# RWKV-7 recursion in a fused transformer block: heads in the two column halves of TensorE's array, two pairs of heads per visit

## The chip, the cores and the metric

The kernel runs on one core of a Trainium2 chip. A core has TensorE (PE; matrix products into PSUM, each with a weight load, PEld), VectorE (DVE), ScalarE (ACT), GpSimd (POOL) and SyncE (SP), which here issues nearly all DMAs. The engines run beside each other and wait for one another by semaphores. The metric is device microseconds of one execution; before the change the median of three runs was 1608.07 us (1606.12 to 1613.35).

## The reference

One layer of an encoder trunk on 256 tokens of width 2048, all in float32: an input projection, two attentions of four heads (stick-breaking and forgetting), an RWKV-7 time mixing with sixteen heads of 64, gated branch products, an output projection and a squared-ReLU MLP of width 8192. What matters here is the recursion of each RWKV head:

```
def frame(state, inp):
    r_t, w_t, k_t, v_t, kk_t, kka_t = inp
    sa = einsum('bhvk,bhk->bhv', state, kk_t)
    state = state * w_t - sa[..., None] * kka_t + v_t[..., None] * k_t
    return state, einsum('bhvk,bhk->bhv', state, r_t)
```

It is a scan over 256 tokens with a 64x64 state in each head.

## The kernel before, in words

**The weight stream.** All large products (GEMMs) read weights in pieces of 128x1024 float32 by DMA. ACT copies each piece to a rounded high part (`whi`, L138), DVE takes the remainder (`wlo`, L139), and TensorE multiplies both parts. In the stage of this change the GEMM is `tok` (L212 for most of it, L197 for the tail of a group): gate and branch products with the tokens in the output's rows. A piece gives eight products with `whi` and four with `wlo`, each 128x128 by 128x512.

**The mixers.** Attention and recursion are a generator, `mixers`, whose pieces are laid between the GEMM's products. `tok` calls `tick` after every four products with `whi` of one weight tile and after every two with `wlo`; `tick` adds credit, and while there is credit it runs the generator up to the next `yield`. A yield ("stage", cost) takes the cost off the credit and ends the tick; I call the work between two such yields a *visit*. When the GEMMs that may go beside the mixers are used up, `while not fin[0]: step()` issues what is left with no ticks. A scheduler then lists each engine's instructions in the order in which it expects them to be ready, so neighbouring pieces can still be shuffled on an engine.

**The recursion.** It runs in two halves of eight heads, four pairs of heads each (`rwkv_half`, PR is the list of pairs). The 256 tokens are cut into four chunks of 64, so a half has 32 triangular systems of 64x64, one for each head and chunk. `SC` holds for each system the score products, `Xt` the values (rows 64 to 128) and the solution (rows 0 to 64), `Bt` and `Kt` the decayed keys and receptances, `Pb` the state of a pair as a block-diagonal 128x128 matrix.

1. DVE inverts the 32x32 diagonal blocks of all systems. Two products of 32x32 per system put the off-diagonal block in place (L626, L633), sixteen systems per visit, four visits; each visit's results are copied by one ACT instruction (L627, L634).
2. Chunk by chunk, five visits for the right-hand sides and the solutions: visit j forms pair j's right-hand side from the state (L652, 64 columns of the array, both heads at once) and the values (L656, per head), and applies the inverse to the right-hand side of pair j-1 (L659, per head). ACT copies both (L662 into `rh`, L664 into `Xt`).
3. Then four visits, one for each pair: the state's update (L670) and the output (L673 from the state, L675 from the solution), each on the whole array for both heads, of whose 128x128 results only the two diagonal 64x64 blocks are used. ACT scales the state (L678), DVE adds the blocks (L682, L684), ACT copies the output blocks (L688).

In a chunk that makes nine visits with a credit of 5 x 0.3 + 4 x 0.6 = 3.9.

Of the kernel before, what the change touches and what calls it, by code (L numbers as in the profile page):

```python
# [49 lines left out]
def hybrid_block(ctx, tc, xt, x, gains, params, consts, lora, gup, wst, out):  # L50
# [244 lines left out]
    ps = mps()  # L295
# [181 lines left out]
    def rwkv_half(hf):  # L477
# [144 lines left out]
        for q in range(2):  # L622
            ps = mps()
            for j in range(16):
                sl = 16 * q + j
                PE.matmul(ps[32:64, j * 32:j * 32 + 32], SC[0:32, sl, 32:64], TW[0:32, sl, :], start=True, stop=True)  # L626
            A.activation(TW[32:64, 16 * q:16 * q + 16, :], ps[32:64].rearrange("p (a b) -> p a b", a=16), AF.Copy)  # L627
            yield ("stage", 0.1)
        for q in range(2):
            ps = mps()  # L630
            for j in range(16):
                sl = 16 * q + j
                PE.matmul(ps[0:32, j * 32:j * 32 + 32], TW[32:64, sl, :], SC[32:64, sl, 32:64], start=True, stop=True)  # L633
            A.activation(SC[0:32, 16 * q:16 * q + 16, 32:64], ps[0:32].rearrange("p (a b) -> p a b", a=16), AF.Copy)  # L634
            yield ("stage", 0.1)
# [7 lines left out]
        for c in range(4):  # L643
            sls = {p: [i * 8 + h * 4 + c for h in range(2)] for i, p in enumerate(PR)}
            rhs = {}

            for j in range(5):
                p, o = PR[j] if j < 4 else None, PR[j - 1] if j else None
                psr = mps() if j < 4 else None
                pso = mps() if j else None  # L650
                if c and j < 4:
                    PE.matmul(psr[0:64, 0:128], Bt[p][:, c, 0:64], Pb[p], start=True, stop=False)  # L652
                for h in range(2):
                    hc = slice(64 * h, 64 * h + 64)
                    if j < 4:
                        PE.matmul(psr[0:64, hc], SC[64:128, sls[p][h], 0:64], Xt[p][64:128, c, hc],  # L656
                                  start=c == 0, stop=c == 0 or h == 1)
                    if j:
                        PE.matmul(pso[0:64, hc], SC[0:64, sls[o][h], 0:64], rhs[o][:, hc], start=True, stop=True)  # L659
                if j < 4:  # L660
                    rhs[p] = rp.tile([64, 128], F32, tag="rh", name=nm("rh"), bufs=4)
                    A.activation(rhs[p], psr[0:64, 0:128], AF.Copy)  # L662
                if j:
                    A.activation(Xt[o][0:64, c, :], pso[0:64, 0:128], AF.Copy)  # L664
                yield ("stage", 0.3)
            for i, p in enumerate(PR):
                X = Xt[p]
                if c < 3:
                    ps = mps()
                    PE.matmul(ps[:, 0:128], Kt[p][:, c, :], X[:, c, :], start=True, stop=True)  # L670
                ps2 = mps()
                if c:
                    PE.matmul(ps2[:, 0:128].rearrange("p (a b) -> p a b", a=2), Pb[p],  # L673
                              Bt[p][:, c:c + 1, 64:128].to_broadcast([128, 2, 64]), start=True, stop=False)
                PE.matmul(ps2[:, 0:128].rearrange("p (a b) -> p a b", a=2), X[:, c, :],  # L675
                          SC[:, sls[p][0]:sls[p][1] + 1:4, 64:128], start=c == 0, stop=True)
                if 0 < c < 3:
                    A.activation(Pb[p], Pb[p], AF.Copy, scale=ecol[:, i, c:c + 1])  # L678
# [7 lines left out]
                for h in range(2):  # L686
                    hr = slice(64 * h, 64 * h + 64)
                    A.activation(y[p][hr, c * 64:c * 64 + 64], ps2[hr, hr], AF.Copy)  # L688
# [580 lines left out]
```

## Time and profile before

| | us |
|---|---|
| median of three runs | 1608.07 |
| the profiled execution | 1608.3 |
| its span, first to last instruction | 1606.5 |
| PE busy | 1562.1 (97%) |
| DVE busy | 1194.4 (74%) |
| ACT busy | 926.7 (58%) |
| first 32x32 product (L626) of the first half | 353.8 |
| first 32x32 product of the second half | 594.9 |

The profile is one execution. PE's rows are matrix products, which are pipelined, so the distance between two starts tells more than their lengths. A float32 product of the recursion appears as two weight loads and two MATMUL records of the same line; I call one such record with its load a *step*. In the trace's rows "64*64" is the part of the array in use (rows times columns), the next figure the output's size in partitions and elements moved. "128*64 128x128" for L652 so means 128 rows and 64 columns of the array with 128 elements moved. Times count from the first instruction.

### The profile page before, as it was taken

How to read it: one execution, taken by the hardware profiler on the slowest of the kernel's cores; microseconds unless marked ns; L12 is line 12 of the kernel's file. 1: busy time of each engine (PE TensorE's matmuls, PEld its weight loads, DVE VectorE, ACT ScalarE, POOL GpSimd, SP SyncE). 2: the span in 40 equal slices, each digit the busy share in tenths (PEclk: the TensorE clock that was granted, in tenths of full speed). 3: DMA queues.
4: the chain of work that ended last, by engine and by line, in shares of the span. 5: the costliest groups of instructions: out<-in, count | busy, mean ns of one | idle time of the engine just before them, and what ended most of it. 6: DMA issues, size and time to landing. Idle time of an engine off the chain costs nothing.

```text
span 1606.5 us, 23353 instructions
## 1 busy us (share of the span) xinstructions
PE 1562.1 (97%) x8846; PEld 1317.1 (82%) x8846; DVE 1194.4 (74%) x1591; ACT 926.7 (58%) x1408; POOL 45.3 (3%) x104
## 2 busy tenths in 40 slices
PE   7999999999999999999999999999899998999997
PEld 7999999997777887788887888887688777878785
DVE  7764558874577884555555778899999999899755
ACT  7474476545675445744444766666666665666442
POOL 0030001000001000000000000000000000000000
PEclk9999999999999999999999999999999999999998
DMA  6646444453445453365685565665466655656564
GB/s 235 209 132 194 148 154 160 148 177 105 136 150 173 156 172 114 103 196 194 204 293 171 169 186 170 209 197 180 164 209 196 202 169 181 200 193 210 168 191 138
DMA packets 94144, 283.38 MB, mean 176 GB/s; under 512 B 9296, under 2 KB 11600, under 8 KB 94032
## 3 DMA queue, kind: packets, MB, share of 16 engines
q1 hardware_dynamic: 91200, 280.66, 53.8%
q8 instruction: 69, 1.13, 0.3%
q10 hardware_dynamic: 2832, 1.24, 0.3%
q14 instruction: 43, 0.35, 0.1%
HBM read 279.77 MB, written 2.10 MB: 175 GB/s over the span
## 4 chain that ended last, share of the span: by engine, by line
PE 83%; DVE 10%; ACT 3%; issue 3%; POOL 1%; DMA 1%; DVEq 0%; SPq 0%; POOLq 0%; ACTq 0%
PE gps L212 29%; PE gps L154 10%; PE gps L197 6%; PE gps L156 6%; PE gps L175 5%; PE gps L176 5%; PE gps L180 5%; DVE wlo L139 3%; DVE raw L1015 2%; PE mps L1047 2%; PE mps L1049 2%; PE mps L1048 2%; ACT whi L138 2%; PE gps L1047 1%; PE gps L1048 1%
## 5 line engine op out<-in xcount | busy, mean ns | idle before, releaser
L139 DVE TENSOR_TENSOR wlo<-raw,whi 128x1024 fp32r<-128x1024 f32 x590 | 716.0, 1222 | 285.6 <-ACT whi L138 235.9
L138 ACT ACTIVATE whi<-raw 128x1024 fp32r<-128x1024 f32 x590 | 619.9, 1057 | 438.0 <-PE gps L212 175.6
L212 PE MATMUL gps<-whi,pk 128*128 128x512 f32 x1144 | 295.4, 396 | 0.0
L212 PEld LDWEIGHTS gps<-whi,pk 128*128 128x128 f32 x1144 | 210.7, 188 | 45.5 <-issue 2.5
L154 PE MATMUL gps<-pk,whi 128*128 128x512 f32 x960 | 244.8, 391 | 0.2 <-ACT whi L138 0.2
L154 PEld LDWEIGHTS gps<-pk,whi 128*128 128x128 f32 x960 | 178.2, 188 | 37.6 <-ACT whi L138 1.1
L212 PE MATMUL gps<-wlo,pk 128*128 128x512 f32 x572 | 160.7, 395 | 0.0
L156 PEld LDWEIGHTS gps<-pk,wlo 128*128 128x128 f32 x1024 | 139.1, 190 | 13.8 <-DVE wlo L139 4.7
L175 PE MATMUL gps<-pk,whi 128*128 128x256 f32 x584 | 148.2, 290 | 0.0
L156 PE MATMUL gps<-pk,wlo 128*128 128x256 f32 x1024 | 143.5, 283 | 1.7 <-DVE wlo L139 1.7
L176 PE MATMUL gps<-pk,whi 128*128 128x256 f32 x584 | 144.5, 283 | 0.0
L212 PEld LDWEIGHTS gps<-wlo,pk 128*128 128x128 f32 x572 | 105.3, 188 | 22.0 <-issue 0.8
L1015 DVE TENSOR_TENSOR raw<-raw,raw 128x1024 f32<-128x1024 f32 x96 | 117.0, 1219 | 0.8
L175 PEld LDWEIGHTS gps<-pk,whi 128*128 128x128 f32 x584 | 112.0, 192 | 2.3 <-issue 1.7
L176 PEld LDWEIGHTS gps<-pk,whi 128*128 128x128 f32 x584 | 112.1, 192 | 0.9 <-issue 0.2
L1047 PE MATMUL mps<-whi,fm 128*128 128x512 f32 x192 | 78.2, 407 | 10.3 <-ACT whi L138 10.0
L180 PE MATMUL gps<-pk,wlo 128*128 128x256 f32 x584 | 82.7, 283 | 0.0
L180 PEld LDWEIGHTS gps<-pk,wlo 128*128 128x128 f32 x584 | 75.6, 192 | 0.0
L1049 PE MATMUL mps<-wlo,fm 128*128 128x512 f32 x192 | 75.2, 392 | 0.0
L1048 PE MATMUL mps<-whi,fm 128*128 128x512 f32 x192 | 75.1, 391 | 0.0
L197 PE MATMUL gps<-whi,pk 128*128 128x512 f32 x264 | 72.2, 396 | 0.0
L972 ACT ACTIVATE tmp<-gps 128x256 f32<-128x256 f32 x64 | 24.4, 381 | 78.3 <-PE gps L158 78.2
(300 smaller groups left out, 1927.0 us busy)
## 6 DMA issues: line engine op xcount, KB each, us to landing
raw<-in_wst_dram SPq DMA_DIRECT2D x518, 512.0 KB, 4.1
x<-in_x_dram SPq DMA_DIRECT2D x8, 256.0 KB, 6.6
out_dram<-x SPq DMA_DIRECT2D x8, 256.0 KB, 2.7
x<-in_xt_dram SPq DMA_DIRECT2D x3, 512.0 KB, 7.4
fm<-in_gains_dram SPq DMA_DIRECT2D x4, 256.0 KB, 5.3
pk<-in_gains_dram SPq DMA_DIRECT2D x4, 256.0 KB, 4.0
con<-in_consts_dram SPq DMA_DIRECT2D x1, 640.0 KB, 8.0
x<-in_xt_dram SPq DMA_DIRECT2D x2, 256.0 KB, 3.6
```

What stands on the lines that cost most here:

```text
L138: A.activation(hi, raw, AF.Copy)
L139: V.tensor_tensor(lo, raw, hi.bitcast(F32), ALU.subtract)
L154: PE.matmul(ps, hi[:, i * 128:i * 128 + 128], pks[i], start=first and i == 0, stop=False)
L156: PE.matmul(ps[:, 0:T], lo[:, i * 128:i * 128 + 128], pks[i][:, 0:T], start=False, stop=False)
L175: PE.matmul(ps[:, 0:T], w, u[:, 0:T], start=h == 0 and i == 0, stop=False)
L176: PE.matmul(ps[:, 0:T], w, u[:, T:2 * T], start=False, stop=False)
L180: PE.matmul(ps[:, 0:T], lo[:, i * 128:i * 128 + 128], pks[8 * h + i][:, 0:T], start=False, stop=h == 1 and i == 7)
L197: PE.matmul(ps[tt], pks[k][:, c:c + 128], w[:, (k - k0) * 512:(k - k0) * 512 + 512], start=k == 0 and part == 0 and w is hl[0], stop=w is ...
L212: PE.matmul(ps[tt], pks[k][:, c:c + 128], w[:, (k - k0) * 512:(k - k0) * 512 + 512], start=k == 0 and part == 0 and w is hl[0], stop=False)
L1015: V.tensor_tensor(R[a], R[a], R[b], ALU.add)
L1047: PE.matmul(Q[f], a, w, start=d == 0 and i == 0, stop=False)
L1048: PE.matmul(Q[f], b, w, start=False, stop=False)
```

## The change

It has three parts, all in `rwkv_half`.

- The 32x32 products are done in two visits of 32 systems instead of four of sixteen. System j goes to column group j % 4 of the array (output partitions 32 x (j % 4) on), and each visit's results are copied by four ACT instructions of 32x256.
- The right-hand sides and solutions are done in three visits, two pairs at a time. The first head of a pair uses columns 0 to 64 of the array, the second head columns 64 to 128, with the output in the matching partitions. The product from the state is one per head now, with 64 moved elements. Four ACT copies bring two pairs' right-hand sides to `rh`; the solutions are copied by DVE, per head, instead of ACT.
- The outputs and the state's update are done in two visits of two pairs. The product from the state (new L684) still uses the whole array but moves 64 elements, as both heads' blocks lie below each other; the products from the solution (new L688) and the update (new L692) are one per head, in the head's column half. The output of a pair is copied by one ACT instruction of 128x64 instead of two.

In a chunk that makes five visits, with the same credit of 3 x 0.5 + 2 x 1.2 = 3.9. The new line numbers are L625 and L632 (32x32 products), L628 and L635 (their copies), L658, L663 and L667 (from the state, from the values, with the inverse), L674 and L676 (copies to `rh` and `Xt`), L684, L688 and L692, L704 (copy of the output).

```diff
-        for q in range(2):
-            ps = mps()
-            for j in range(16):
-                sl = 16 * q + j
-                PE.matmul(ps[32:64, j * 32:j * 32 + 32], SC[0:32, sl, 32:64], TW[0:32, sl, :], start=True, stop=True)
-            A.activation(TW[32:64, 16 * q:16 * q + 16, :], ps[32:64].rearrange("p (a b) -> p a b", a=16), AF.Copy)
-            yield ("stage", 0.1)
...
+        ps = mps()
+        for j in range(32):
+            PE.matmul(ps[32 * (j % 4):32 * (j % 4) + 32, j // 4 * 32:j // 4 * 32 + 32], SC[0:32, j, 32:64],
+                      TW[0:32, j, :], start=True, stop=True)
+        for g in range(4):
+            A.activation(TW[32:64, g:32:4, :], ps[32 * g:32 * g + 32, 0:256].rearrange("p (a b) -> p a b", a=8), AF.Copy)
+        yield ("stage", 0.2)
...
-            for j in range(5):
-                p, o = PR[j] if j < 4 else None, PR[j - 1] if j else None
...
-                if c and j < 4:
-                    PE.matmul(psr[0:64, 0:128], Bt[p][:, c, 0:64], Pb[p], start=True, stop=False)
-                for h in range(2):
-                    hc = slice(64 * h, 64 * h + 64)
-                    if j < 4:
-                        PE.matmul(psr[0:64, hc], SC[64:128, sls[p][h], 0:64], Xt[p][64:128, c, hc],
-                                  start=c == 0, stop=c == 0 or h == 1)
-                    if j:
-                        PE.matmul(pso[0:64, hc], SC[0:64, sls[o][h], 0:64], rhs[o][:, hc], start=True, stop=True)
-                if j < 4:
-                    rhs[p] = rp.tile([64, 128], F32, tag="rh", name=nm("rh"), bufs=4)
-                    A.activation(rhs[p], psr[0:64, 0:128], AF.Copy)
-                if j:
-                    A.activation(Xt[o][0:64, c, :], pso[0:64, 0:128], AF.Copy)
-                yield ("stage", 0.3)
...
+            for j in range(3):
+                ps, os = PR[2 * j:2 * j + 2], PR[2 * j - 2:2 * j] if j else []
+                psr = [mps(), mps()] if ps else None
+                pso = mps() if os else None
+                if c:
+                    for i, p in enumerate(ps):
+                        for hc in HC:
+                            PE.matmul(psr[i][hc, 0:64], Bt[p][:, c, 0:64], Pb[p][:, hc],
+                                      start=True, stop=False)
+                for i in range(2):
+                    for h, hc in enumerate(HC):
+                        if ps:
+                            PE.matmul(psr[i][hc, 0:64], SC[64:128, sls[ps[i]][h], 0:64],
+                                      Xt[ps[i]][64:128, c, hc], start=c == 0, stop=True)
+                    for h, hc in enumerate(HC):
+                        if os:
+                            PE.matmul(pso[hc, 64 * i:64 * i + 64], SC[0:64, sls[os[i]][h], 0:64],
+                                      rhs[j - 1][:, i, hc], start=True, stop=True)
+                for hc in HC:
+                    if ps:
+                        if j not in rhs:
+                            rhs[j] = rp.tile([64, 2, 128], F32, tag="rh", name=nm("rh"), bufs=2)
+                        for i in range(2):
+                            A.activation(rhs[j][:, i, hc], psr[i][hc, 0:64], AF.Copy)
+                    for i, o in enumerate(os):
+                        V.tensor_copy(Xt[o][0:64, c, hc], pso[hc, 64 * i:64 * i + 64])
+                yield ("stage", 0.5)
...
-                if c:
-                    PE.matmul(ps2[:, 0:128].rearrange("p (a b) -> p a b", a=2), Pb[p],
-                              Bt[p][:, c:c + 1, 64:128].to_broadcast([128, 2, 64]), start=True, stop=False)
-                PE.matmul(ps2[:, 0:128].rearrange("p (a b) -> p a b", a=2), X[:, c, :],
-                          SC[:, sls[p][0]:sls[p][1] + 1:4, 64:128], start=c == 0, stop=True)
...
+                if c:
+                    for i, p in enumerate(PR[2 * j:2 * j + 2]):
+                        PE.matmul(psy[i][:, 0:64], Pb[p], Bt[p][:, c, 64:128], start=True, stop=False)
+                for i, p in enumerate(PR[2 * j:2 * j + 2]):
+                    X = Xt[p]
+                    for h, hc in enumerate(HC):
+                        PE.matmul(psy[i][hc, 0:64], X[:, c, hc], SC[:, sls[p][h], 64:128],
+                                  start=c == 0, stop=True)
+                    for hc in HC:
+                        if c < 3:
+                            PE.matmul(psp[hc, 64 * i:64 * i + 64], Kt[p][:, c, hc], X[:, c, hc], start=True, stop=True)
...
+                yield ("stage", 1.2)
```

How it moves TensorE's instructions shows at three places. In these rows a product stands once (not as two records), its tile numbers are the program's, and the sizes at the end are output partitions by moved elements. First the 32x32 products of the first half, before:

```order
L626 MATMUL mps_4045<-TW_3981,SC_2612 32x32 x16
L212 MATMUL gps_3969<-wlo_4014,pk_532 128x512
L212 MATMUL gps_3970<-wlo_4014,pk_532 128x512
L626 MATMUL mps_4065<-TW_3981,SC_2612 32x32 x16
L212 MATMUL gps_3969<-whi_4031,pk_600 128x512 x2
L212 MATMUL gps_3970<-whi_4031,pk_600 128x512 x2
L633 MATMUL mps_4093<-SC_2612,TW_3981 32x32 x16
```

and in the change:

```order
L625 MATMUL mps_4045<-TW_3981,SC_2612 32x32 x32
L212 MATMUL gps_3969<-wlo_4014,pk_532 128x512
L212 MATMUL gps_3970<-wlo_4014,pk_532 128x512
L212 MATMUL gps_3969<-whi_4031,pk_600 128x512
L632 MATMUL mps_4084<-SC_2612,TW_3981 32x32 x2
L212 MATMUL gps_3969<-whi_4031,pk_600 128x512
L212 MATMUL gps_3970<-whi_4031,pk_600 128x512
L632 MATMUL mps_4084<-SC_2612,TW_3981 32x32
L212 MATMUL gps_3970<-whi_4031,pk_600 128x512
L632 MATMUL mps_4084<-SC_2612,TW_3981 32x32 x29
```

The first batch is one visit now; the second, which needs all four copies of the first, is cut into three by GEMM products (in the second half it is whole). Then chunk 2 of the first half, from the last visit for its solutions on, in the change:

```order
L663 MATMUL mps_4465<-Xt_3402,SC_2612 64x64 x2
L667 MATMUL mps_4466<-rh_4453,SC_2612 64x64 x2
L212 MATMUL gps_4413<-wlo_4418,pk_386 128x512
L212 MATMUL gps_4414<-wlo_4418,pk_386 128x512
L667 MATMUL mps_4490<-rh_4479,SC_2612 64x64 x4
L212 MATMUL gps_4413<-whi_4435,pk_454 128x512 x2
L212 MATMUL gps_4414<-whi_4435,pk_454 128x512 x2
L212 MATMUL gps_4413<-whi_4435,pk_459 128x512 x2
L212 MATMUL gps_4414<-whi_4435,pk_459 128x512 x2
L212 MATMUL gps_4413<-wlo_4436,pk_454 128x512
L212 MATMUL gps_4414<-wlo_4436,pk_454 128x512
L684 MATMUL mps_4516<-Bt_2652,Pb_4131 128x64
```

Visits are fewer and farther apart, but between the second and the third visit for the right-hand sides only two GEMM products stand here; the output visit, which was on the whole array throughout, now begins on the whole array (L684) and goes on in its column halves. Last the end of the second half, where no ticks are left, in the change:

```order
L658 MATMUL mps_6674<-Pb_6236,Bt_5139 64x64 x2
L663 MATMUL mps_6674<-Xt_5662,SC_5093 64x64 x2
L212 MATMUL gps_6832<-whi_6612,pk_308 128x512
L658 MATMUL mps_6675<-Pb_6239,Bt_5278 64x64 x2
L663 MATMUL mps_6675<-Xt_5669,SC_5093 64x64 x2
L212 MATMUL gps_6832<-whi_6612,pk_308 128x512
L212 MATMUL gps_6833<-whi_6612,pk_308 128x512
L658 MATMUL mps_6689<-Pb_6242,Bt_5424 64x64
L212 MATMUL gps_6833<-whi_6612,pk_308 128x512
```

Chunk 3 stands here, visit upon visit with single GEMM products between; before, the outputs of chunk 2 stood here too.

More of the change, by code (lines that the diff above doesn't have):

```diff
@@ L666, in rwkv_half @@
-            for i, p in enumerate(PR):
-                X = Xt[p]
+            HC = (slice(0, 64), slice(64, 128))
+            for j in range(3):
[25 more added lines that the diff above has]
+                yield ("stage", 0.5)
@@ L668, in rwkv_half @@
+            for j in range(2):
                 if c < 3:
-                    ps = mps()
-                    PE.matmul(ps[:, 0:128], Kt[p][:, c, :], X[:, c, :], start=True, stop=True)
-                ps2 = mps()
+                    psp = mps()
+                psy = [mps(), mps()]
                 if c:
-                    PE.matmul(ps2[:, 0:128].rearrange("p (a b) -> p a b", a=2), Pb[p],
-                              Bt[p][:, c:c + 1, 64:128].to_broadcast([128, 2, 64]), start=True, stop=False)
```

42 lines of the change are left out of this document (20 added, 22 removed).

## The prediction

> **What bounds the kernel now.** I read the page's head first, then the busy time in stretches, then TensorE's timeline.
>
> ```profile
> span 1606.5 us, 23353 instructions
> PE 1562.1 (97%) x8846; PEld 1317.1 (82%) x8846; DVE 1194.4 (74%) x1591; ACT 926.7 (58%) x1408; POOL 45.3 (3%) x104
> ```
>
> The change touches two places only, the end of each half of the RWKV recursion. The first 32x32 product starts at 353.8 us, those of the second half at 594.9. The stretches there:
>
> ```profile
> core 0: us, PE busy (x) PEld busy (x) DVE busy (x) ACT busy (x) POOL busy (x), PEclk, DMA share, GB/s
> 353.80:362.30 8.50, 8.50 (x143) 6.64 (x142) 1.24 (x2) 4.41 (x6) 0.00 (x0) 1.00 0.58 187
> 362.30:420.00 57.70, 57.70 (x372) 42.64 (x372) 23.58 (x39) 29.84 (x84) 0.42 (x2) 1.00 0.34 110
> 600.00:660.00 60.00, 59.35 (x379) 43.30 (x378) 24.43 (x44) 34.47 (x93) 0.00 (x0) 1.00 0.25 82
> ```
>
> TensorE has no gap here (57.70 of 57.70 us) at the full granted clock, while DVE and ACT are near half busy and the DMA engines at a third. So what a visit of the recursion takes on TensorE is paid in full by the span, and what is saved there is gained in full, as long as no new wait appears. The whole prediction is therefore a count of TensorE time in these two stretches.
>
> **The prices, from TensorE's timeline.** Columns: start, length, then the instruction; every product is two MATMUL records here.
>
> ```profile
> 349.63 1.07 PE L212 MATMUL gps<-whi,pk 128*128 128x512 f32 x4
> 350.54 1.07 PE L212 MATMUL gps<-wlo,pk 128*128 128x512 f32 x4
> ...
> 355.59 1.19 PE L626 MATMUL mps<-TW,SC 32*32 32x32 f32 x32
> 356.72 1.19 PE L212 MATMUL gps<-whi,pk 128*128 128x512 f32 x4
> 357.83 1.19 PE L633 MATMUL mps<-SC,TW 32*32 32x32 f32 x32
> ...
> 362.33 0.44 PE L656 MATMUL mps<-Xt,SC 64*64 64x64 f32 x4
> 362.70 1.19 PE L212 MATMUL gps<-whi,pk 128*128 128x512 f32 x4
> 363.82 0.27 PE L656 MATMUL mps<-Xt,SC 64*64 64x64 f32 x1
> 363.83 0.27 PE L659 MATMUL mps<-rh,SC 64*64 64x64 f32 x1
> 363.93 0.22 PE L656 MATMUL mps<-Xt,SC 64*64 64x64 f32 x1
> 363.93 0.22 PE L659 MATMUL mps<-rh,SC 64*64 64x64 f32 x1
> 363.99 0.22 PE L656 MATMUL mps<-Xt,SC 64*64 64x64 f32 x1
> 363.99 0.22 PE L659 MATMUL mps<-rh,SC 64*64 64x64 f32 x1
> 364.04 0.22 PE L656 MATMUL mps<-Xt,SC 64*64 64x64 f32 x1
> ```
>
> The weight product (GEMM) steps at (350.54 - 349.63)/4 = 0.2275 us. A 32x32 step: the last of 32 starts one length (0.19) before the group ends, so (1.19 - 0.19)/31 = 0.032 us. A 64x64 step is 0.055 us (363.93, 363.99, 364.04). And L656 and L659, which read the lower and the upper 64 rows of the array, run side by side: two steps in each 0.055 us.
>
> Then the price of changing the array's division. The visit of sixteen 32x32 products takes 357.83 - 355.59 - 4 x 0.2275 = 1.33 us, 32 steps make 1.02, and 0.31 is left for two changes (into the visit and out of it). The four-step visit takes 363.82 - 362.33 - 0.91 = 0.58 us, steps 0.22, so 0.36 for two. Two more visits:
>
> ```profile
> 386.01 0.38 PE L670 MATMUL mps<-Xt,Kt 128*128 128x128 f32 x2
> 386.23 0.39 PE L673 MATMUL mps<-Bt,Pb 128*128 128x128 f32 x2
> 386.45 0.39 PE L675 MATMUL mps<-SC,Xt 128*128 128x128 f32 x2
> 386.60 1.17 PE L212 MATMUL gps<-whi,pk 128*128 128x512 f32 x4
> ...
> 394.35 0.43 PE L652 MATMUL mps<-Pb,Bt 128*64 128x128 f32 x2
> 394.72 0.27 PE L656 MATMUL mps<-Xt,SC 64*64 64x64 f32 x1
> ...
> 395.10 1.19 PE L212 MATMUL gps<-whi,pk 128*128 128x512 f32 x4
> 396.21 0.43 PE L652 MATMUL mps<-Pb,Bt 128*64 128x128 f32 x2
> ```
>
> A 128x128 step is (386.23 - 386.01)/2 = 0.11 us, and those visits need no change, since the GEMM uses the whole array too. The visit at 394.35 takes 396.21 - 394.35 - 0.91 = 0.95 us: two steps of L652 (64 columns loaded, 128 moving; at 0.11) and four of 0.055 make 0.44, and 0.51 is left for three changes. I take **0.17 us a change**.
>
> **Before, summed.** 256 steps of L626 and L633 x 0.032 = 8.2; 48 of L652 x 0.11 = 5.3; 40 right-hand-side visits of four step lengths each x 0.055 = 8.8; 160 of L670, L673 and L675 x 0.11 = 17.6: 39.9 us. Along the instruction order the division changes 117 times: 19.9 us. Together 59.8 us.
>
> **After.** The steps are mostly the same in number and half as wide. L625 and L632: 256. L658: 96, with 64 columns loaded and 64 moving, like L656, 0.055. L663 and L667: 24 visits whose longer row half has eight steps, 192 lengths. L688 128 and L692 96, 0.055 each. L684, 48: it loads 128 columns and moves 64; no row shows this, the bounds are 0.055 and 0.11, and L652 shows that the wider operand decides, so 0.11, 5.3 us. The changes are counted at 118, not fewer: there are fewer visits, but the output visits now leave the whole-array division (two changes each), and the order cuts visits apart in two places. So the changes add 0.2 us, and everything hangs on one thing that the trace doesn't show: whether products in different **column** groups run side by side as those in different row halves do.
>
> - None side by side: 8.2 + 5.3 + 10.6 + 12.3 (L688, L692) + 5.3 = 41.7, that is +1.8, with the changes +2.0 us.
> - All side by side: the 32-wide fall to a quarter (2.05), the 64-wide to a half (2.65, 5.3, 6.15), L684 stays at 5.3: 21.45, that is -18.45, with the changes -18.2 us.
>
> I take the column halves as fully side by side, since the rows of L656 and L659 show that two tiles of the array each load and multiply within one 0.055 us. For the 32-wide steps I take half, 0.016 us: those rows show 0.0275 us a step with two running, a quarter of 0.032 would be 0.008, and no row shows TensorE starting steps that densely. Their term is then 4.1 instead of 2.05, and the sum 39.9 - 23.5 = 16.4 saved, less 0.2: **-16.2 us**.
>
> One page speaks against it. The Trainium skill, TensorE: Matmul & The Clock Gate, section Part 3: Packing small matmuls, says that a weight load overlaps running products only where the row group differs, which would leave +2.0 us in place of -16.2; the same section reports three column groups at 2.38 times the speed of one. The trace agrees on the rows (363.82 and 363.83) and has nothing on columns.
>
> **New waits.** The copies out of PSUM change shape.
>
> ```profile
> L662 ACT ACTIVATE rh<-mps 64x128 f32<-64x128 f32 x32 | 8.6, 270 | 22.4 <-PE mps L659 18.1 <-PE mps L656 3.5
> L688 ACT ACTIVATE g<-mps 64x64 f32<-64x64 f32 x64 | 13.8, 215 | 2.9 <-PE mps L675 2.1
> L682 DVE TENSOR_SCALAR Pb<-mps,ecol 64x64 f32<-64x64 f32 x16 | 4.5, 283 | 7.4 <-PE mps L670 7.0
> L972 ACT ACTIVATE tmp<-gps 128x256 f32<-128x256 f32 x64 | 24.4, 381 | 78.3 <-PE gps L158 78.2
> L138 ACT ACTIVATE whi<-raw 128x1024 fp32r<-128x1024 f32 x590 | 619.9, 1057 | 438.0 <-PE gps L212 175.6 <-PE gps L176 65.2 <-DVE raw L1015 58.4
> ```
>
> A visit's right-hand sides now need four ACT copies, 4 x 0.215 = 0.86 us, before the next visit's L667 can start; before it was one, 0.27. With about 0.3 us around them (an estimate: the 0.22 that a product lasts and a start), 1.15 us must be covered by GEMM between two visits. Four GEMM steps and the change give about 1.1, two give 0.63. In the change's order three of the sixteen such gaps hold two steps and one holds three, so about 3 x 0.5 + 0.3 = 1.8 us of waiting with the 0.05 of the gaps of four taken as nothing. TW and SC each need four copies of 32x256, at most the 0.381 of L972's form each, 1.5 us, against a gap of about 2 us in the first half and six steps (1.5 us) in the second: 0.2 us. Behind a waiting L667 stands the next GEMM, so these waits are paid. The copies of Xt go from ACT to DVE, eight of about 0.283 us a chunk, 18 us of DVE over both stretches, beside 23.58 of 57.70 busy: hidden, though the weight remainders (wlo, L139) stand behind them in DVE's queue, and what that costs if the cover fails is the 1.14 us of four copies for each GEMM group. At the end of the second half the recursion outlasts its GEMM in both kernels; there chunk 3 has five dependent visits with little cover, about 1 us more. Nothing below zero is to be had here, as the copies lie behind products. Sum: +2.7 us, bounds 0 and 8 (0.35 us on each of sixteen gaps and the two TW batches, plus the end).
>
> **Sum.** -16.2 + 2.7 = -13.5 us. The profiled execution took 1608.3 us (1606.5 of span and 1.8 around it), 0.2 above the median of 1608.07, so 1608.3 - 13.5 = 1594.8, **1595 us**.
>
> **Rivals.**
> - *Column groups don't run side by side.* Two records of one product follow each other in one tile, and if TensorE starts the next tile's product only after them, nothing is gained: +2.0 + 2.7, **1613 us**. This is also what the page's rule on row groups would do here. For it: no row shows two column groups at once. Against it: the two row halves are independent although their products are paired too.
> - *The copies decide, slower.* Each L667 and L632 waits for four ACT copies; where a weight copy L138 (1.057 us) stands in ACT's queue before them, the visit is late by up to that. On eighteen such places 0.7 us each is 12.6; with +2.0 from steps one after another it is +14.6, **1623 us**. It decides from a mean wait of 0.35 us on, where it passes +8. With the column halves side by side the same waits would leave -16.2 + 12.6, 1605 us. Against it: ACT is busy 29.84 of 57.70 us, and TensorE has no gap in that stretch although L659 waits for L662's copies there too. The Trainium skill, TensorEngine Tiling (Array Packing), section PSUM Bottleneck, warns that tiling quickens TensorE but not the copies out of PSUM; so far the trace shows room for them.
> - *The halves overlap, the 32-wide groups don't.* The 4.1 us is lost: 1599 us, inside the forecast's range.
>
> **How the numbers follow.** Forecast with its variant 0.58, no overlap 0.28, copies decide 0.14. About 0.5%, 8 us, is what a measurement of this kernel tells from no change: below 1600 is faster, above 1616 slower. The forecast's own range is 1588 (all side by side, -18.2, no waits, and L684 at its lower bound, -2.65) to 1604 (waits at 8 and the 32-wide term lost), of which 0.04 falls within 0.5%. No overlap falls within it (0.25) but for 0.03 above; the copies' rival gives 0.11 above and 0.03 within. So faster 0.54, same 0.32, slower 0.14. The range, 1588 to 1615, leaves out about 0.03 below, and above the copies' rival and a part of no overlap, 0.16.
>
> **What would show it.** In the timeline after, L663's two heads should start within 0.01 us of each other, as L656 and L659 do now, and the 32 products of L625 should last about 1.0 us instead of 2.0. If L625's row is 2.0 us long and L688 steps by 0.055 with nothing beside it, the first rival holds. Changes should cost 0.17 us still. If TensorE shows idle time in front of L667 or L632 of over 5 us in all, the copies decide. The prediction is wrong if the column halves share one stream, or if the two stretches shorten and the GEMM behind them then waits for wlo or DMA.

## The result, and the profile after

| | before | after |
|---|---|---|
| median | 1609.84 us (4 runs, 1606.12 to 1613.35) | 1594.53 us (4 runs, 1593.31 to 1595.01) |
| ratio of times, 95% interval | | 0.9905 [0.9891, 0.9919] |
| the profiled execution | 1608.3 us | 1594.32 us |
| its span | 1606.5 us | 1592.2 us |

The change gains 0.95%, 15.3 us in the medians and 14.3 us in the spans. The page of the changed kernel begins:

```profile
span 1592.2 us, 23684 instructions
PE 1548.0 (97%) x9006; PEld 1305.8 (82%) x9006; DVE 1205.7 (76%) x1655; ACT 918.7 (58%) x1384; POOL 44.5 (3%) x104
```

TensorE is busy for 14.1 us less, with 160 records more (the per-head products); so the gain is TensorE's, as the prediction counted it. Busy time by stretches of the changed kernel (start and end, length, then busy time of PE, PEld, DVE, ACT and POOL, the granted clock, DMA share, GB/s):

```profile
351.57:361.70 10.13, 9.42 (x166) 6.42 (x166) 1.64 (x4) 6.42 (x18) 0.00 (x0) 0.66 0.50 157
361.70:416.40 54.70, 54.70 (x454) 42.28 (x453) 30.13 (x70) 26.77 (x69) 0.84 (x4) 1.00 0.39 126
592.00:651.00 59.00, 59.00 (x455) 43.26 (x453) 33.95 (x80) 32.93 (x78) 0.00 (x0) 1.00 0.34 109
```

Both chunk stretches are still without a gap, although DVE now holds the copies into `Xt`. New is the first row: around the 32x32 products TensorE lacks 0.71 us of 10.13, and its granted clock is 0.66 on the mean. The timeline of that place (start, length, instruction, and in brackets the idle time before it and what ended it):

```profile
351.57 0.75 PE L625 MATMUL mps<-TW,SC 32*32 32x32 f32 x64
352.25 0.73 PE L212 MATMUL gps<-wlo,pk 128*128 128x512 f32 x2
352.82 0.40 PE L212 MATMUL gps<-whi,pk 128*128 128x512 f32 x1
353.77 0.24 PE L632 MATMUL mps<-SC,TW 32*32 32x32 f32 x2 [0.55 <-ACT TW L628]
354.17 0.24 PE L632 MATMUL mps<-SC,TW 32*32 32x32 f32 x2 [0.16 <-ACT TW L628]
...
356.06 1.06 PE L632 MATMUL mps<-SC,TW 32*32 32x32 f32 x58
...
357.67 2.07 PE L212 MATMUL gps<-whi,pk 128*128 128x512 f32 x4
359.54 1.05 PE L212 MATMUL gps<-wlo,pk 128*128 128x512 f32 x2
```

L625's 64 records last 0.75 us: the last starts 0.55 us after the first (0.75 less one length of 0.2), 0.0087 us a record instead of 0.032. And the four GEMM records from 357.67 on take (359.54 - 357.67)/4 = 0.47 us each instead of 0.2275, because the clock is at a half there.

What the second batch waits for stands in ACT's timeline of the same place:

```profile
352.26 1.06 ACT L138 ACTIVATE whi<-raw 128x1024 fp32r<-128x1024 f32 x1 [1.88 <-DMA raw<-in_wst_dram]
353.34 1.58 ACT L628 ACTIVATE TW<-mps 32x256 f32<-32x256 f32 x4
```

A weight copy (L138) starts just as the first batch ends and stands before the four copies, which then come one after another, 0.40 us apart. The first L632 (353.77) starts right after the first copy, the second (354.17) right after the second. So each product waits for the copy of its own column group, not for all four, and by these times the three GEMM products would have covered the first copy without the 1.06 us of L138 ahead of it.

The second place is the chunk loop:

```profile
374.38 0.45 PE L658 MATMUL mps<-Pb,Bt 128*64 128x64 f32 x8
374.76 0.27 PE L663 MATMUL mps<-Xt,SC 64*64 64x64 f32 x2
374.77 0.27 PE L667 MATMUL mps<-rh,SC 64*64 64x64 f32 x2
374.87 0.22 PE L663 MATMUL mps<-Xt,SC 64*64 64x64 f32 x2
374.88 0.23 PE L667 MATMUL mps<-rh,SC 64*64 64x64 f32 x2
374.93 0.23 PE L663 MATMUL mps<-Xt,SC 64*64 64x64 f32 x2
...
376.74 0.45 PE L667 MATMUL mps<-rh,SC 64*64 64x64 f32 x8
377.12 0.73 PE L212 MATMUL gps<-wlo,pk 128*128 128x512 f32 x2
377.69 0.55 PE L684 MATMUL mps<-Bt,Pb 128*128 128x64 f32 x4
378.17 0.34 PE L688 MATMUL mps<-SC,Xt 128*64 128x64 f32 x4
...
```

The "x2" are the two column halves: four records, two row halves by two column halves, in each 0.055 us (374.87 to 374.93), where the kernel before had two.

**Where the time went.** The weight products (GEMM) are the same 6608 records in every kernel here, so I set the start of the same GEMM record in one trace against the other; each stretch holds the same GEMM products, and the first row begins at the first of them, the last ends at the start of the last. These are my sums over records, in us:

| GEMM records | what lies there | before | after |
|---|---|---|---|
| 0 to 2300 | all before the first half's 32x32 products | 344.74 | 343.20 |
| 2300 to 2480 | first half: 32x32 products and chunks | 71.69 | 65.39 |
| 2480 to 3090 | between | 163.46 | 164.67 |
| 3090 to 3275 | second half | 80.83 | 73.73 |
| 3275 to the end | all behind it | 925.78 | 925.85 |

The two halves give -6.3 and -7.1, together -13.4 of the 14.3 us. The -1.5 ahead of them is one half-clock stretch of 3.4 us at 185 us that the profiled execution of before had and this one hadn't. The +1.2 between holds the same records, in 40 turns between GEMM and other work instead of 36. The remaining -0.7 lies ahead of the first GEMM record, which starts 8.53 us into the span before and 7.83 after.

### The profile page after: what moved, and what is told of

Its sections match the earlier page's. It is cut to its first block, busy times and chain, and to the rows that moved or that the text cites. A ratio compares the mean times of both kernels' runs of the same rounds, so it can differ in the third digit from the quotient of the medians.

```text
span 1592.2 us, 23684 instructions
## 1 busy us (share of the span) xinstructions
PE 1548.0 (97%) x9006; PEld 1305.8 (82%) x9006; DVE 1205.7 (76%) x1655; ACT 918.7 (58%) x1384; POOL 44.5 (3%) x104
## 4 chain that ended last, share of the span: by engine, by line
PE 82%; DVE 10%; ACT 3%; issue 2%; DMA 1%; POOL 1%; SPq 0%; DVEq 0%; ACTq 0%; POOLq 0%
PE gps L212 29%; PE gps L154 10%; PE gps L197 6%; PE gps L156 6%; PE gps L175 5%; PE gps L180 5%; PE gps L176 5%; DVE wlo L139 3%; DVE raw L1031 2%; PE mps L1063 2%; PE mps L1065 2%; PE mps L1064 2%; ACT whi L138 2%; PE gps L1063 1%; PE gps L1064 1%
## 5 line engine op out<-in xcount | busy, mean ns | idle before, releaser
L138 ACT ACTIVATE whi<-raw 128x1024 fp32r<-128x1024 f32 x590 | 620.0, 1057 | 451.4 <-PE gps L212 183.9
```

Source lines behind the costliest of these rows:

```text
L138: A.activation(hi, raw, AF.Copy)
```

## The experiments

All ratios are against the kernel before, run beside them. Differences to the changed kernel are taken between medians of different rounds, in which the median of the kernel before was 1609.84, 1609.35 and 1609.88 us.

### Which part gives what

**e1**: only the 32x32 products and their copies are changed, the chunks are those of before.

```diff
-        for q in range(2):
-            ps = mps()
-            for j in range(16):
-                sl = 16 * q + j
-                PE.matmul(ps[32:64, j * 32:j * 32 + 32], SC[0:32, sl, 32:64], TW[0:32, sl, :], start=True, stop=True)
...
+        for j in range(32):
+            PE.matmul(ps[32 * (j % 4):32 * (j % 4) + 32, j // 4 * 32:j // 4 * 32 + 32], SC[0:32, j, 32:64],
+                      TW[0:32, j, :], start=True, stop=True)
...
```

> Only the 32x32 products changed (two visits in four column groups, copies by four ACT instructions); right-hand sides and outputs as in the kernel before. Theory (column groups run side by side): the 64 records of L625 last about 0.75 us as in the changed kernel, so the four batches save about 6 us of steps; against that stand the waits for the four copies (about 1 us) and, if it is they that bring it, a stretch of 6.8 us at half clock in the first half (about 3 us). So 2 to 6 us below the kernel before, 0.9963 to 0.9988 of it. Rival (fewer visits are what saves, not the columns): two visits of about 0.33 us less in each half, the cut takes that back; within 1 us of the kernel before.

**e2**: only the chunks are changed, the 32x32 products are those of before (the diff is against the changed kernel, as all that follow are).

```diff
-        for j in range(32):
-            PE.matmul(ps[32 * (j % 4):32 * (j % 4) + 32, j // 4 * 32:j // 4 * 32 + 32], SC[0:32, j, 32:64],
-                      TW[0:32, j, :], start=True, stop=True)
...
+        for q in range(2):
+            ps = mps()
+            for j in range(16):
+                sl = 16 * q + j
+                PE.matmul(ps[32:64, j * 32:j * 32 + 32], SC[0:32, sl, 32:64], TW[0:32, sl, :], start=True, stop=True)
...
```

> Only the column halves and the two pairs per visit; the 32x32 products as in the kernel before. Theory: L658, L663, L667, L688 and L692 run two heads side by side, 12 us of steps saved less 1 to 2 us of waits: 10 to 11 us below the kernel before, ratio 0.993 to 0.994, and no half clock at 355 us. Rival (the waits for the copies eat it): under 6 us below.

Measured: e1 1605.84 us against 1609.35, ratio 0.998 [0.9971, 0.999]; e2 1597.59, ratio 0.9932 [0.9918, 0.9947]. The gains, 3.5 and 11.8 us, add up to the whole change's 15.3. In e1 the two halves' stretches fall by 0.5 and 2.1 us only, though its 32x32 records take 3.9 us where they took 8.0: the first half shows the wait that the changed kernel has, too (0.73 us), and 3.4 us at half clock right behind it, from 359.4 us on. e2 has no half clock near 355 us, as expected, but 3.4 us of it in the second half, at 592.2. The first batch and the second in e1's timeline:

```profile
353.85 0.75 PE L625 MATMUL mps<-TW,SC 32*32 32x32 f32 x64
...
356.07 0.24 PE L632 MATMUL mps<-SC,TW 32*32 32x32 f32 x2 [0.57 <-ACT TW L628]
```

**e3**: the changed kernel with right-hand sides and solutions all in columns 0 to 64; the outputs keep their column halves.

```diff
-                        for hc in HC:
-                            PE.matmul(psr[i][hc, 0:64], Bt[p][:, c, 0:64], Pb[p][:, hc],
-                                      start=True, stop=False)
+                        PE.matmul(psr[i][0:64, 0:128], Bt[p][:, c, 0:64], Pb[p], start=True, stop=False)
...
-                            PE.matmul(psr[i][hc, 0:64], SC[64:128, sls[ps[i]][h], 0:64],
-                                      Xt[ps[i]][64:128, c, hc], start=c == 0, stop=True)
+                            PE.matmul(psr[i][0:64, hc], SC[64:128, sls[ps[i]][h], 0:64],
+                                      Xt[ps[i]][64:128, c, hc], start=c == 0, stop=c == 0 or h == 1)
...
-                            PE.matmul(pso[hc, 64 * i:64 * i + 64], SC[0:64, sls[os[i]][h], 0:64],
+                            PE.matmul(pso[0:64, 128 * i + 64 * h:128 * i + 64 * h + 64], SC[0:64, sls[os[i]][h], 0:64],
...
```

> The changed kernel with its visits and copies, but the right-hand sides and solutions of both heads in the array's columns 0 to 64 (the product from the state as one per pair with 128 moved elements, as before the change). Theory (columns side by side): 24 visits lose four step lengths of 0.055 us, and the products from the state 2.6 us: about 8 us above the changed kernel, some 6 us below the kernel before. Rival (fewer visits are what saves): no more than 1 us above the changed kernel.

**e4**: the changed kernel with all 32x32 products in one column group.

```diff
-            PE.matmul(ps[32 * (j % 4):32 * (j % 4) + 32, j // 4 * 32:j // 4 * 32 + 32], SC[0:32, j, 32:64],
+            PE.matmul(pq[j % 4 // 2][32:64, 256 * (j % 2) + j // 4 * 32:256 * (j % 2) + j // 4 * 32 + 32], SC[0:32, j, 32:64],
                       TW[0:32, j, :], start=True, stop=True)
...
```

> The changed kernel with its visits and copies, but all 32x32 products in one column group (outputs in two banks). Theory: the 64 records of a batch last 2.0 us instead of 0.75, so 5 to 6 us above the changed kernel. Rival (the column groups give nothing there, two visits do): within 1 us of the changed kernel.

Measured: e3 1598.68 us, ratio 0.9937 [0.9923, 0.9952]; e4 1597.99, ratio 0.9932 [0.9917, 0.9946]. They give back 4.2 and 3.5 us of the gain, less than the 8 and the 5 to 6 expected. The timeline of e3 (L661 is the change's L663, L665 its L667):

```profile
375.17 0.22 PE L661 MATMUL mps<-Xt,SC 64*64 64x64 f32 x1
375.18 0.22 PE L665 MATMUL mps<-rh,SC 64*64 64x64 f32 x1
375.23 0.22 PE L661 MATMUL mps<-Xt,SC 64*64 64x64 f32 x1
375.24 0.22 PE L665 MATMUL mps<-rh,SC 64*64 64x64 f32 x1
```

And the row of e4 that answers to L625 above:

```profile
351.54 2.21 PE L625 MATMUL mps<-TW,SC 32*32 32x32 f32 x64
```

In one column half there are two records per 0.06 us again, and 64 records of 32x32 last 2.21 us instead of 0.75. With the visits and the number of copies of the changed kernel kept, only the place in the columns is taken away (in e3 the product from the state is one per pair again, too), so the overlap of column groups is shown for both sizes. Summed over both halves, start to start inside a visit, e3's 64x64 records take 11.9 us instead of 7.1, and e4's 32x32 records 8.1 instead of 4.1. Over the stretches of both halves and what lies between (records 2300 to 3275) e3 takes 3.5 us more than the changed kernel, the balance of three things: its right-hand sides and solutions, with the changes out of them, cost 6.2 us more; it happens to have 13 changes of division fewer at the uncovered end, which saves about 1.0 on the changes into the visits; and its half-clock stretch near 357 us is 3.4 us long instead of 6.8, about 1.7 less. e4 takes 4.8 us more there: its records cost 4.0, a second half-clock stretch (3.4 us at 592.4) about 1.7, and it lacks the 1.1 us of waits for TW, since its slower batch gives the copies time.

### What the change leaves behind

**f1**: two empty visits between the two batches of 32x32 products, so that GEMM comes between them.

```diff
             A.activation(TW[32:64, g:32:4, :], ps[32 * g:32 * g + 32, 0:256].rearrange("p (a b) -> p a b", a=8), AF.Copy)
         yield ("stage", 0.2)
+        yield ("stage", 0.1)
+        yield ("stage", 0.1)
```

> The changed kernel with two empty visits between the two batches of 32x32 products (two more yields of 0.1), so that GEMM products cover the copies into TW and the second batch is not cut. Theory (the wait for the copies, and the low activity around it, bring the stretch of half clock at 355 us): no idle time before L632, four changes of division fewer, and no half clock between 350 and 365 us: 3 to 4.5 us below the changed kernel. Rival (the half clock comes at that place by chance): only the idle time and the changes go, 1 to 1.5 us below, and a half clock stretch still appears there.

Measured: 1588.04 us, ratio 0.9862 [0.9847, 0.9876], 6.5 us below the changed kernel. The second batch (here L634) is whole and waits for nothing:

```profile
352.94 0.75 PE L625 MATMUL mps<-TW,SC 32*32 32x32 f32 x64
353.62 0.73 PE L212 MATMUL gps<-wlo,pk 128*128 128x512 f32 x2
354.19 2.00 PE L212 MATMUL gps<-whi,pk 128*128 128x512 f32 x8
356.02 0.61 PE L212 MATMUL gps<-wlo,pk 128*128 128x512 f32 x2
356.57 0.75 PE L634 MATMUL mps<-SC,TW 32*32 32x32 f32 x64
```

The first half's stretch falls from 65.39 to 61.03 us. Of these 4.4 us the wait is 0.7, three changes fewer (50 instead of 53) are 0.5, and the remaining 3.1 is what 6.8 us at half clock had cost. The second half gains 1.6 us as well (72.13 instead of 73.73), which the theory had left out; so the whole is more than the 3 to 4.5 expected.

**f2**: smaller credits for the visits, so that the second half's last chunk comes while there is GEMM to lie under.

```diff
-                yield ("stage", 0.5)
+                yield ("stage", 0.4)
...
-                yield ("stage", 1.2)
+                yield ("stage", 0.8)
```

> The changed kernel with smaller credits for the new visits (0.4 and 0.8 instead of 0.5 and 1.2), so that chunk 3 of the second half still lies between GEMM products. Theory (the uncovered end costs its cut visits, 13 changes of 0.16 us, and some waits): the second half's stretch is 2 to 4 us shorter. Rival (the end is paid by the same TensorE work either way): within 1 us of the changed kernel.

Measured: 1591.0 us, ratio 0.9881 [0.9866, 0.9895], 3.5 below the changed kernel. The last outputs of the second half in the changed kernel:

```profile
633.20 0.33 PE L688 MATMUL mps<-SC,Xt 128*64 128x64 f32 x2
633.46 0.50 PE L212 MATMUL gps<-wlo,pk 128*128 128x512 f32 x1
633.89 0.34 PE L688 MATMUL mps<-SC,Xt 128*64 128x64 f32 x4
634.15 0.50 PE L212 MATMUL gps<-wlo,pk 128*128 128x512 f32 x1
634.58 0.33 PE L688 MATMUL mps<-SC,Xt 128*64 128x64 f32 x2
```

And in f2:

```profile
618.39 0.55 PE L684 MATMUL mps<-Bt,Pb 128*128 128x64 f32 x4
618.87 0.45 PE L688 MATMUL mps<-SC,Xt 128*64 128x64 f32 x8
619.25 0.73 PE L212 MATMUL gps<-wlo,pk 128*128 128x512 f32 x2
```

With no ticks left, single GEMM products cut the visit to pieces and each piece pays two changes; the changed kernel has 73 changes in that stretch. In f2 the visit is whole. Over the three stretches from record 2300 to 3275 (work moves between them here) before takes 315.98 us, the changed kernel 303.79 and f2 299.81, the last two both with 6.8 us at half clock near 355. They make 158 and 143 changes there; at 0.16 us the 15 fewer are 2.4 of the 4.0 us, and where the rest comes from is not shown.

**f3**: both, and the output's product from the state (L684) in column halves as well.

```diff
-                        PE.matmul(psy[i][:, 0:64], Pb[p], Bt[p][:, c, 64:128], start=True, stop=False)
+                        for hc in HC:
+                            PE.matmul(psy[i][hc, 0:64], Pb[p][:, hc], Bt[p][:, c, 64:128], start=True, stop=False)
...
```

> The changed kernel with all three: the two empty visits, the smaller credits, and L684 in the column halves too (one product per head with 64 columns loaded, in place of one per pair on the whole array). The last saves about 0.8 us a half by the steps (24 records of 0.093 and a change of 0.205 six times against 48 of 0.032). Sum of the theories: 6 to 9 us below the changed kernel, near 1587 us. Rival (half clock by chance, end paid anyway): 2 to 3 us below.

Measured: **1581.86 us** (1580.96 to 1584.86), ratio 0.9828 [0.9812, 0.9844], the best here and more than the 6 to 9 us expected; the three stretches take 291.79 us, 12.0 less than in the changed kernel, where f1 gains 6.4 and f2 4.0. So about 1.6 us remain for the product from the state, which no run changes alone. An output visit in it (L687 is the change's L684, L691 its L688):

```profile
383.32 0.45 PE L687 MATMUL mps<-Bt,Pb 128*64 128x64 f32 x8
383.61 0.29 PE L691 MATMUL mps<-SC,Xt 128*64 128x64 f32 x4
```

The product takes 0.29 us there instead of 0.48 (377.69 to 378.17). The change of division that stood behind it is not saved, it now stands in front: the product starts 0.32 us after the last GEMM record before it, instead of 0.23. Counted from that GEMM record to the next one behind the visit, less 0.2275, a visit with update takes 0.94 us instead of 1.10.

### Do the copies decide, and what brings the half clock

**f4**: every copy of the right-hand sides to `rh` done twice on ACT.

```diff
                             A.activation(rhs[j][:, i, hc], psr[i][hc, 0:64], AF.Copy)
+                            A.activation(rhs[j][:, i, hc], psr[i][hc, 0:64], AF.Copy)
```

> The changed kernel with every copy into rh done twice on ACT (the same values). Theory (the copies are covered by GEMM but for the gaps of two products): each of 16 gaps has 0.86 us more to cover, those of two and three products wait 0.9 longer, those of four 0.6: 6 to 10 us above the changed kernel. Rival (copies don't decide at all, GEMM covers them twice over): within 2 us.

Measured: 1598.74 us over ten runs that spread widely (1593.84 to 1607.8), ratio 0.9941 [0.9919, 0.9962]. The copies to `rh` among ACT's groups from 350 to 420 us (operation, shapes, count, busy time, mean ns, idle time before) in the changed kernel:

```profile
L674 ACT ACTIVATE rh<-mps 64x64 f32<-64x64 f32 x32 | 6.5, 218 | 4.4 <-PE mps L663 3.9
```

The same in f4:

```profile
L675 ACT ACTIVATE rh<-mps 64x64 f32<-64x64 f32 x32 | 5.9, 216 | 0.3
L674 ACT ACTIVATE rh<-mps 64x64 f32<-64x64 f32 x32 | 5.9, 214 | 3.0 <-PE mps L663 2.6
```

And the whole list of what TensorE waited for in f4 from 350 to 420 us (total, times, longest; idle time between records):

```profile
PE mps L632 <- ACT TW L628: 0.7, 2, 0.5
```

That is 32 copies more in the half, over 5 us of ACT, and still TensorE sits idle before no L667. The order gives way instead: later visits are cut by GEMM, 61 and 81 changes instead of 53 and 73. The stretches grow by about 2.0 and 1.2 us over those of the changed kernel without its half clock. So the copies are covered, with little to spare. The median lies 4.2 us above the changed kernel, between the theory (6 to 10) and its rival (2), and most of the spread goes with the clock: the two runs above 1607 us have a mean granted clock of 0.984 and 0.985, the two fastest, at 1594 us, 0.995 and 0.994. Why f4 has so much more half clock in some runs no profile shows; that stays open.

**g1, g2, g3**: the changed kernel again, f1 again, and the changed kernel with each copy of the first 32x32 batch (L628) done twice:

```diff
             A.activation(TW[32:64, g:32:4, :], ps[32 * g:32 * g + 32, 0:256].rearrange("p (a b) -> p a b", a=8), AF.Copy)
+            A.activation(TW[32:64, g:32:4, :], ps[32 * g:32 * g + 32, 0:256].rearrange("p (a b) -> p a b", a=8), AF.Copy)
```

> The changed kernel itself, once more. In its first profile the granted clock fell to 0.50 for 6.8 us at 354.9 us, right behind the second 32x32 batch that waits for its copies; the prediction had no such term. If the waiting batch brings it on (theory), it is here again between 350 and 365 us, 3.4 or 6.8 us long. If it falls by chance (rival), it may as well be gone: the other single half-clock stretches of the kernels so far fall at places that differ from run to run. Stretches of RWKV as before: 65.4 and 73.7 us of TensorE time with it, about 62 for the first without it.

> The changed kernel with two empty visits between the two 32x32 batches, once more: the second batch comes when its copies are long done. Theory: no half clock between 350 and 365 us, first stretch about 61 us. Rival (chance): a half-clock stretch there may turn up here as well, and the first stretch would be 63 to 65 us.

> The changed kernel with every copy of the first 32x32 batch (L628) done twice on ACT, so that the second batch L632 comes about 1 to 1.5 us later. Theory: TensorE waits 1 us or more before L632 in both halves, and half clock follows at about 355 us and perhaps at about 592 us too; the time is 2 to 6 us above the changed kernel's. Rival: the wait alone is paid, 1 to 2 us, and where half clock falls has nothing to do with it.

Measured (one execution each, no interval): g1 1594.38 us, g2 1587.62, g3 1593.76. The busy time in stretches of 3.41 us (columns as above, the granted clock the third from the end) in the first profile of the changed kernel:

```profile
351.45:354.86 3.41, 2.70 (x74) 1.69 (x73) 1.42 (x2) 2.50 (x5) 0.00 (x0) 1.00 0.87 257
354.86:358.27 3.41, 3.41 (x72) 2.40 (x72) 0.00 (x0) 1.16 (x4) 0.00 (x0) 0.50 0.64 214
358.27:361.69 3.42, 3.42 (x23) 2.33 (x22) 0.34 (x2) 2.75 (x11) 0.00 (x0) 0.50 0.01 4
```

In g1:

```profile
353.82:357.23 3.41, 3.20 (x77) 2.25 (x78) 0.86 (x1) 1.88 (x6) 0.00 (x0) 1.00 0.75 253
357.23:360.64 3.41, 3.41 (x23) 2.28 (x23) 0.63 (x4) 3.12 (x11) 0.00 (x0) 0.50 0.17 65
```

And in g3:

```profile
354.20:357.60 3.40, 2.98 (x20) 1.95 (x21) 0.82 (x1) 2.75 (x9) 0.00 (x0) 1.00 0.78 241
357.60:361.00 3.40, 3.24 (x80) 1.78 (x79) 0.71 (x4) 3.28 (x10) 0.00 (x0) 1.00 0.18 65
```

The half clock is back in g1, half as long, and absent in g2, as my theory said. But it is absent in g3, where the second batch waits for 0.65 us, and in f4, where it waits as in the changed kernel; and e4 has it at 356.9 and 592.4 us with no wait at all. **So the wait doesn't bring it on; that theory falls.** g3's time, within a microsecond of the changed kernel's, shows no price of the slower copies either: GEMM and L664 (the change's L663) moved into the wait.

What the thirteen profiles do share is a lack of GEMM. Take the fewest GEMM records that start in any 3.41 us around the two 32x32 batches of a half. It is 2 to 5 in the two halves of the ten kernels without the gap (before too: 3), and in 8 of these 20 places half clock followed. It is 6 to 8 in f1, g2 and f3, and half clock followed in none of their 6. Whether a place is hit hangs in part on where a window of the clock falls. All half-clock stretches of one execution ahead of the last 25 us lie whole multiples of 3.413 us apart (g1: 149, 231, 282 and 333 times from the first), so they lay a grid over each trace. In each of the 8 places the window of that grid right ahead of the half clock holds 3 to 5 GEMM records; no window at full clock near the batches with 6 or more was followed by half clock. But 5 windows with 4 or 5 were not followed by it either (two in before, one each in e2, f2 and g3), so the count alone doesn't decide. This is a pattern over profiles and not an experiment on the clock; what the chip counts as activity stays open.

## Why the prediction was right

It said 1595 us and 13.5 us less than before; the median is 1594.53, the spans differ by 14.3 and the medians by 15.3. That the time fits to half a microsecond is in part luck, since the kernel before stood at 1608.07 when the sum was made and at 1609.84 beside the change. By its own steps:

**What bounds the kernel.** Right. What TensorE saves in the two stretches is gained: 13.4 of the 14.3 us lie there.

**The prices and the sum before.** Right. A change still costs about what it did. The visit at 376.74 takes 377.69 - 376.74 - 2 x 0.2275 = 0.50 us, eight steps of 0.0275 make 0.22, and 0.28 is left for two changes, 0.14 each; the visit at 374.38 has six GEMM products up to 376.74, 2.36 - 1.37 = 0.99 us less 0.44 for its steps, 0.18 for each of three. The prediction took 0.17. It counted 117 and 118 changes; the traces have 125 and 126 with the eight of the group norm. Without GEMM and the rows of the group norm the two stretches of before hold 62.0 us, counted were 59.8. (One reading was off without harm: 594.9 us is where the last L626 of the second half starts; the first starts at 592.1.)

**Column halves side by side.** Right, and this was the step that everything hung on: the rows at 374.76 and 374.77, and e3 for the cause. The page that spoke against it (the Trainium skill, TensorE: Matmul & The Clock Gate, Part 3: Packing small matmuls) lets a weight load overlap only where the row group differs; L658's eight records use all 128 rows in both column halves, and the last starts (0.45 - 0.23) = 0.22 us after the first, 0.03 us a record where a step on its own was put at 0.055. The measurement decides against the rule here. The first rival (no overlap, 1613 us) is out.

**32-wide groups at half the gain.** Too cautious: 0.0087 us a record in L625, 0.0096 over all in f1, near the quarter of 0.032 that the forecast would not take. In the changed kernel the term still came to 4.1 us for the two batches as predicted, but for another reason, since the second batch is cut and partly at half clock; f1 has it at 2.4. The third rival is out with e4.

**L684 at 0.11 us.** Measured 0.093, 0.8 us less in all. That the visit has two changes of division was counted right, and f3 doesn't save them; it saves on the steps.

**New waits, +2.7 us.** Mis-sized. (Its parts, 1.8, 0.2 and 1, add up to 3.0; the forecast stays 1595 with that.) 1.8 us was taken for right-hand sides that come late; TensorE is never idle there (59.00 of 59.00 us busy in the second half's row), and f4 shows that even twice the copies aren't seen as idle time. The step that failed is that an L667 needs all four copies. At a gap of two GEMM products in the changed kernel:

```profile
389.74 0.95 ACT L674 ACTIVATE rh<-mps 64x64 f32<-64x64 f32 x4
390.42 0.65 PE L667 MATMUL mps<-rh,SC 64*64 64x64 f32 x8
```

The first L667 starts at 390.42 us, before the last copy ends (390.69), as each product reads one copy only. What is left of the wait shows as records farther apart: the eight last 0.65 us instead of 0.45, so 0.2 us at this gap, as much at another (620.82) and nothing at the third (604.28), where 0.5 each was expected. The wait for TW was put at 0.2 us and is 0.71 and 0.38: the sum took a gap of 2 us in the first half, but before the first L632 stand three GEMM products, 0.7 us, and L138 delays the copies. Less the 0.65 us that before spent on the group norm and after does not, that is 0.4 net of idle time, 0.8 with the records spread apart, instead of 2.7. The rival in which the copies decide (1623 us) is out, though its mechanism, a weight copy ahead in ACT's queue, is there at one place, the first TW batch. The end of the second half was taken as a wait of 1 us; there is none, but the cuts cost changes (f2).

**What the prediction had no term for.** The clock. It took the granted clock of before, 1.00, as given, and 6.8 us at half clock near 355 us cost about 3.1 us. So the right sum owes something to two errors that cancel: waits about 2 us too dear, and no half clock. Without it the two stretches would have given 16.5 us, or 16.9 without the waits too; the steps and changes alone had been put at 16.2.

## What to carry to other kernels

When an engine has no gap, count its records by their start-to-start distance and put the price of switching between shapes beside that of the steps; here the switches were a third of the work's time and did not fall at all. Small products that don't fill the array belong side by side in its columns too, not only in its rows: 64-wide pairs went to half and 32-wide groups of four to about a quarter of their time. A batch that waits for the copies of the one before it wants other work between; in the profiles here no half clock followed a 32x32 batch where six or more GEMM records stood in every 3.41 us around it.

## What the hardware showed that was not expected

- Records of 32x32 start every 0.0087 us when they go round four column groups; the densest of before were 0.0275 apart on the mean.
- Half clock comes without idle time: e4 at 589.0 to 592.4 us has no TensorE wait above 0.02 us, and the clock is 0.50 from 592.4 on. All such stretches ahead of the last 25 us are 3.413 or 6.827 us long. The Trainium skill, TensorE: Matmul & The Clock Gate, Part 1: The HAM clock gate, names a free-running window of 3413 ns, and the trace agrees with that number; it names an idle window as what takes the clock down, and here it went down behind windows in which TensorE was busy, with many small products and few of the GEMM.
- The same kernel's profiles differ in where half clock falls (g1 has it at five places ahead of the last 25 us, 17.1 us in all, the first profile at two, 13.7 us, at nearly the same time, 1594.38 and 1594.32 us).
